# Two more blocks of the dilated values by quads of half products, and the combinations of x formed piece by piece

## The chip, the cores and the metric

The kernel runs on one core of one Trainium2 chip. The metric is the device time of one execution in microseconds (us), as the median over several runs. The engines are TensorE (PE in the rows; its weight loads are PEld), VectorE (DVE), ScalarE (ACT), GpSimd (POOL) and SyncE (SP), each of which takes its own instructions in the order in which they stand.

## The reference

A trunk of two layers over 512 tokens of width 1024, all in f32: forgetting attention with 16 heads, then dilated window attention with 3 groups of 8 heads of width 128, each followed by a gated embedding, and a norm at the end. The change lies in the input projection of the dilated layer:

```python
def dilated_mixer(h, w_in, w_out):
    B, S, _ = h.shape
    proj = h @ w_in
    shp = (B, S, DIL_GROUPS, DIL_HEADS_PER_GROUP, DIL_HEAD_DIM)
    q = proj[..., :DIL_QKV].reshape(shp)
    k = proj[..., DIL_QKV:2 * DIL_QKV].reshape(shp)
    v = proj[..., 2 * DIL_QKV:3 * DIL_QKV].reshape(shp)
    z = proj[..., 3 * DIL_QKV:]
```

The values v of a group are a product of x (512 tokens by 1024 features, after the norm) with 1024 columns of `w_in`.

## The kernel before

Every f32 operand of a projection is split into a rounded part and a remainder (`whi` and `wlo` for weights; x has the same two parts in the pair of tiles `xn2T`), and a product is three matmuls: high by high, high by low, low by high. ScalarE makes the high part of a weight, VectorE the low part by a subtraction.

The dilated layer runs in two halves, `hf` 0 and 1, of four heads each. A half begins with three blocks of values, one for each group g, of 512 columns each, called (hf, g) here; then come, for each of its four heads j, the queries and keys of three groups (`pair_rows`), and in places gates (`gate_rows`). There are two ways to compute a block of values:

- `token_rows`: the plain product. Four granules of weights (256 features by 512 columns), and for each granule four blocks of 128 tokens; one unit is 6 matmuls of 128x512, so a block is 96 of them. The four sums lie in four PSUM banks, and are copied to `v` by VectorE (even ones, line 1059) and ScalarE (odd ones, line 1057) after the last granule.
- `quad_rows`: a Strassen-like scheme, with seven half products in place of eight. `Stream.quad` makes seven combinations of the quarters a11, a12, a21, a22 of the weight block (VectorE sums of lines 144, 145, 149 and 156) and splits each of them (lines 135 and 136). Each of seven products is 24 matmuls of 128x256, so a block is 168 of them. The products are called after the parts of x that they take: "11", "t2", "t1", "t3", "21", "t4", "22", in this order. Sums between products go through three temporaries p1, u2, u4 in `ozf`.

The parts t1 to t4 of x are combinations of its four quarters. `combine_x` forms them once: four sums of high and low parts into `xf`, four differences, and four splits into the pair of tiles `comb` (12 steps on VectorE, 4 on ScalarE). Before the change it is called after the blocks (0, 0) and (0, 1) were issued, and `QUADS` names the blocks (0, 2), (1, 1) and (1, 2); the queries, keys and gates use `comb` too.

A scheduler orders the instructions of each engine from this program by what it reckons to be ready; the order in the program is only its priority. `Side` holds short pieces of work that are run at a later unit (`tick`); `chain` holds the generators of a head's scores and values (`dil_scores`, `dil_values`), of which `drive` runs a step after each unit. A generator's step ends at a `yield`.

Two things that the prediction also speaks of: at the start of the layer GpSimd builds three tables of distances, `d0`, `d1` and `d2` (lines 861 to 872; the last takes 32 selects one after the other), and VectorE makes from them the biases of each head (lines 911 to 913, in `dil_scores`), those of head 0 being free to run as soon as the tables are there. And the scores of a head send row sums to DRAM and back (`own` to `sta` and `stb`, then to `oth`) through SyncE's queue, in which the weight loads (line 73, at most three raw granules at a time) stand too; `dil_values` turns them into the factors `alpha` (lines 969 to 977), scales the probabilities (lines 980 and 981), transposes them (line 995) and multiplies with the values (lines 1006 to 1012).

Of the kernel before, what the change touches and what calls it, by code (L numbers as in the profile page):

```python
# [19 lines left out]
OP = mybir.AluOpType  # L20
# [8 lines left out]
def f32(ap):  # L29
    return ap.bitcast(F32)  # L30
# [3 lines left out]
def trunk_kernel(ctx, tc, x, p, fox_norm, fox_w_in, fox_b_f, fox_w_out, dil_norm, dil_w_in,  # L34
                 dil_w_out, ple_w_up, ple_w_gate, final_norm, out):
    nc = tc.nc
    PE, ACT, DVE, POOL, SP = nc.tensor, nc.scalar, nc.vector, nc.gpsimd, nc.sync
# [158 lines left out]
    g_fo = [tok_granules(fox_w_out[0], c * 512) for c in range(2)]  # L196
    g_g0 = [tok_granules(ple_w_gate[0], c * 512) for c in range(2)]
    g_up1 = [ws.add(ple_w_up[1], 0, 2, c * 512, 512) for c in range(2)]
    QUADS = ((0, 2), (1, 1), (1, 2))
    g_dv, g_dq, g_dk, g_dz = {}, {}, {}, {}  # L200
    z_after = {0: (0, 1), 2: (2, 3), 4: (4, 5), 7: (6, 7)}
    for hf in range(2):
        for g in range(3):
            c0 = 6144 + g * 1024 + hf * 512
            if (hf, g) in QUADS:
                g_dv[hf, g] = [ws.add(dw, k, 4, c0 + c, 256) for k, c in ((0, 256), (0, 0), (4, 256), (4, 0))]
# [34 lines left out]
    side = Side()  # L241
# [3 lines left out]
    def step(n=1):  # L245

        for _ in range(n):
            while chain:
                try:
                    next(chain[0])  # L250
                    break
                except StopIteration:
                    chain.popleft()

    def drive(main, steps=1, at={}):


        for i, _ in enumerate(main):
            side.tick()
            step(steps if isinstance(steps, int) else steps[i])  # L260
            if i in at:
                at[i]()
# [116 lines left out]
    def quad_rows(xb, i0, pool, temps, v):  # L379

        combos = ws.quad(i0, pool)
        ready = deque()
        b1, b2, b3, b4 = (rotate(mm) for _ in range(4))
        p1, u2, u4 = temps

        def dst(cols, h):
            return v[:, 2 * h:2 * h + 2, 256 * cols:256 * cols + 256]

        def halves(t):
            return t.rearrange("p (r c) -> p r c", r=2)  # L390

        def product(o, n, first):

            while len(ready) < 5:
                c = next(combos, None)
                if c is None:
                    break
                ready.append(c)
            wh, wl = ready.popleft()
            for r in range(2):  # L400
                oo = o[:, r * 256:(r + 1) * 256]
                for k in range(4):
                    xh, xl = (a[:, k, r * P:(r + 1) * P] for a in xb[n])
                    PE.matmul(oo, xh, wh[:, k, :], start=first and r == 0 and k == 0, stop=False,
                              skip_group_check=True)
                    PE.matmul(oo, xh, wl[:, k, :], start=False, stop=False, skip_group_check=True)
                    PE.matmul(oo, xl, wh[:, k, :], start=False, stop=(k == 3), skip_group_check=True)

        product(b1, "11", True)
        ACT.activation(p1, b1, AF.Copy)  # L410
        yield
        product(b2, "t2", True)
        DVE.tensor_tensor(u2, b2, p1, OP.add)
        yield
        product(b4, "t1", True)
        DVE.tensor_tensor(u4, b4, u2, OP.add)
        yield
        product(b3, "t3", True)
        DVE.tensor_tensor(dst(1, 1), halves(b3), halves(u4), OP.add)
        yield  # L420
        product(b1, "21", False)
        ACT.activation(dst(0, 0), halves(b1), AF.Copy)
        yield
        product(b3, "t4", False)
        DVE.tensor_tensor(dst(1, 0), halves(b3), halves(u2), OP.add)
        yield
        product(b4, "22", False)
        DVE.tensor_tensor(dst(0, 1), halves(b4), halves(u2), OP.add)
        yield

# [2 lines left out]
    def split_out(hi, lo, src):  # L433
        last["act"] = ACT.activation(hi, src, AF.Copy)  # L434
        DVE.tensor_tensor(lo, src, f32(hi), OP.subtract)
# [417 lines left out]
    dp = dil.enter_context(tc.tile_pool(name="dil", bufs=1))  # L853
    xT = xn2T[0]
# [3 lines left out]
    for r in range(4):  # L858
        d = d0[32 * r:32 * r + 32]
# [11 lines left out]
    for n in range(32):  # L871
# [9 lines left out]
    xb = {f"{i + 1}{h + 1}": [a[:, 4 * i:4 * i + 4, 256 * h:256 * h + 256] for a in xT]  # L881
          for i in range(2) for h in range(2)}
# [10 lines left out]
        return lambda h: (d[:, 256 * h:256 * h + 256], lambda t: t)  # L893

    def combine_x():
        xf = dp.tile([P, 4, 4, 256], F32, tag="ozf", bufs=1, name="xf")
        b11, b12, b21, b22 = (xf[:, i] for i in range(4))
        for n, d in (("11", b11), ("12", b12), ("22", b22), ("21", b21)):
            DVE.tensor_tensor(d, f32(xb[n][0]), f32(xb[n][1]), OP.add)
        DVE.tensor_tensor(b11, b12, b11, OP.subtract)  # L900
        DVE.tensor_tensor(b12, b22, b12, OP.subtract)
        DVE.tensor_tensor(b22, b22, b11, OP.subtract)
        DVE.tensor_tensor(b21, b21, b22, OP.subtract)
        for n, d in (("t1", b11), ("t2", b22), ("t3", b12), ("t4", b21)):
            split_out(xb[n][0], xb[n][1], d)

    def dil_scores(j, st):
        bias0 = dp.tile([P, 256], F32, tag="bias0", bufs=1, name=nm("bias0"))
# [142 lines left out]
    for hf in range(2):  # L1051
        v = [dp.tile([P, NB, 512], F32, tag=f"v{g}", bufs=1, name=nm("v"))
             for g in range(3)]
        for g in range(3):
            def dv_evac(b, t, g=g, v=v):
                if b % 2:
                    ACT.activation(v[g][:, b, :], t, AF.Copy)
                else:
                    DVE.tensor_copy(v[g][:, b, :], t)
            if hf == 0 and g == QUADS[0][1]:  # L1060
                combine_x()
                ozf = dp.tile([P, 8, T], F32, tag="ozf", bufs=1, name="ozf")
            if (hf, g) in QUADS:
                drive(quad_rows(xb, g_dv[hf, g][0], dp, [ozf[:, n, :] for n in (5, 6, 7)], v[g]))
            else:
                drive(token_rows(xT, g_dv[hf, g], blk, dv_evac))
            if g == 0:
                to_blocks(v[0])
        for j in range(4 * hf, 4 * hf + 4):
            st = {"q": [], "k": [], "v": v}  # L1070
            for g in range(3):
                views = []
                for n, nme in enumerate("qk"):
                    d = qk[:, 2 * g + n, :]
                    if g:
                        d = d.rearrange("p (r i) -> p r i", r=4)
                    st[nme].append(d)
                    views.append(by_residue(qk[:, 2 * g + n, :]) if g else by_block(d))
                drive(pair_rows(xb, g_dq[j, g], g_dk[j, g], dp, *views))
            if j < 7:  # L1080
                finish()
                chain.extend((dil_scores(j, st), dil_values(j, st)))
            else:
                chain.appendleft(dil_scores(j, st))
                chain.append(dil_values(j, st))
            if j in z_after:
                drive(gate_rows(*z_after[j]), (0,) + (1,) * 6)
# [59 lines left out]
```

## Time and profile before

| | |
|---|---|
| median of 3 runs | 967.32 us (966.49 to 968.38) |
| the profiled execution | 967.62 us, its span 965.6 us |
| granted TensorE clock, mean | 0.996 |
| TensorE busy / weight loads | 97% / 87% of the span |
| VectorE, ScalarE, GpSimd busy | 72%, 51%, 6% |
| DMA | 104.56 MB, mean 108 GB/s |

All times in rows are microseconds from the start of the span. A busy TensorE only says that its pipeline was never empty; how fast it ran shows in the distance between the starts of matmuls. The span leaves out some 2 us around it.

### The profile page before, as it was taken

The numbers are of one execution on the slowest core, as the hardware profiler recorded it, in microseconds if no ns is written. First come the engines' busy times: TensorE is split into PE (matmuls) and PEld (weight loads), VectorE is DVE, ScalarE is ACT, GpSimd is POOL, SyncE is SP. The second block draws the span as 40 slices with busy tenths as digits, with TensorE's granted clock in tenths as the row PEclk, the third lists the DMA queues.
The fourth block names the chain that finished last, engine by engine and source line by source line (L and its number), as shares of the span: only waits on it lengthen the run. The fifth ranks groups of instructions, "written<-read, shape, count | busy, mean of one in ns | idle before, by whom it ended". The sixth has DMA issues, their size and how long they took to land. (4 is left out here: it accounts for less than half of the span.)

```text
span 965.6 us, 15587 instructions
## 1 busy us (share of the span) xinstructions
PE 939.6 (97%) x5928; PEld 840.9 (87%) x5928; DVE 695.9 (72%) x1416; ACT 494.9 (51%) x915; POOL 54.7 (6%) x103
## 2 busy tenths in 40 slices
PE   6999999999999999899999999999999999999996
PEld 5888888888888888789999999999999999997885
DVE  5765877777764478758888887657888897666445
ACT  6455777777752246334464555444355455464233
POOL 0000000000010000920000000010000000000000
PEclk9999999999999999999999999999999999999998
DMA  8453222221246227253333323335332322345302
GB/s 293 124 153 88 67 67 67 66 67 66 67 153 218 87 90 259 66 154 87 113 85 88 78 77 95 104 113 147 91 110 68 110 71 72 99 156 200 128 1 87
DMA packets 127355, 104.56 MB, mean 108 GB/s; under 512 B 16528, under 2 KB 105616, under 8 KB 127280
## 3 DMA queue, kind: packets, MB, share of 16 engines
q1 hardware_dynamic: 123008, 90.65, 31.5%
q0 software_dynamic: 4096, 12.65, 3.9%
q8 instruction: 46, 0.75, 0.3%
q14 instruction: 29, 0.24, 0.1%
q10 hardware_dynamic: 176, 0.26, 0.1%
HBM read 92.93 MB, written 10.55 MB: 107 GB/s over the span
## 5 line engine op out<-in xcount | busy, mean ns | idle before, releaser
L87 DVE TENSOR_TENSOR wlo<-wraw,whi 128x1024 fp32r<-128x1024 f32 (+1 forms) x82 | 99.5, 1214 | 102.2 <-ACT whi L86 101.7
L86 ACT ACTIVATE whi<-wraw 128x1024 fp32r<-128x1024 f32 (+1 forms) x82 | 85.7, 1047 | 100.4 <-PE ps L300 62.2
L347 PE MATMUL ps<-comb,whi 128*128 128x256 f32 x448 | 131.2, 293 | 0.0
L349 PE MATMUL ps<-comb,wlo 128*128 128x256 f32 x448 | 126.8, 283 | 0.0
L348 PE MATMUL ps<-comb,whi 128*128 128x256 f32 x448 | 126.7, 283 | 0.0
L347 PE MATMUL ps<-xn2T,whi 128*128 128x256 f32 x336 | 97.1, 289 | 0.0
L349 PE MATMUL ps<-xn2T,wlo 128*128 128x256 f32 x336 | 95.0, 283 | 0.0
L348 PE MATMUL ps<-xn2T,whi 128*128 128x256 f32 x336 | 95.0, 283 | 0.0
L108 ACT ACTIVATE whi<-ws 128x1024 fp32r<-128x1024 f32 x56 | 59.2, 1057 | 68.2 <-PE ps L348 59.5
L348 PEld LDWEIGHTS ps<-comb,whi 128*128 128x128 f32 x448 | 85.8, 192 | 0.4
L347 PEld LDWEIGHTS ps<-comb,whi 128*128 128x128 f32 x448 | 85.8, 192 | 0.4
L349 PEld LDWEIGHTS ps<-comb,wlo 128*128 128x128 f32 x448 | 85.7, 191 | 0.0
L328 PE MATMUL ps<-xnT,whi 128*128 128x512 f32 x192 | 78.5, 409 | 0.0
L109 DVE TENSOR_TENSOR wlo<-ws,whi 128x1024 fp32r<-128x1024 f32 x56 | 68.4, 1221 | 11.8 <-ACT whi L108 11.6
L330 PE MATMUL ps<-xnT,wlo 128*128 128x512 f32 x192 | 75.5, 393 | 0.0
L329 PE MATMUL ps<-xnT,whi 128*128 128x512 f32 x192 | 75.1, 391 | 0.0
L108 ACT ACTIVATE whi<-wraw 128x1024 fp32r<-128x1024 f32 (+1 forms) x56 | 47.2, 843 | 34.4 <-issue 12.4
L348 PEld LDWEIGHTS ps<-xn2T,whi 128*128 128x128 f32 x336 | 64.4, 192 | 0.0
L347 PEld LDWEIGHTS ps<-xn2T,whi 128*128 128x128 f32 x336 | 64.4, 192 | 0.0
L349 PEld LDWEIGHTS ps<-xn2T,wlo 128*128 128x128 f32 x336 | 64.3, 191 | 0.0
L109 DVE TENSOR_TENSOR wlo<-wraw,whi 128x1024 fp32r<-128x1024 f32 (+1 forms) x56 | 52.8, 950 | 0.2 <-ACT whi L108 0.2
L298 PE MATMUL ps<-whi,ozT 128*128 128x512 f32 x128 | 51.0, 400 | 1.0 <-ACT ozT L434 1.0
(242 smaller groups left out, 2422.3 us busy)
## 6 DMA issues: line engine op xcount, KB each, us to landing
wraw<-in_dil_w_in_dram SPq DMA_DIRECT2D x80, 512.0 KB, 3.7
wraw<-in_fox_w_in_dram SPq DMA_DIRECT2D x32, 512.0 KB, 4.1
wraw<-in_ple_w_gate_dram SPq DMA_DIRECT2D x16, 512.0 KB, 4.1
up_dram<-upo SPq DMA_DIRECT2D x16, 256.0 KB, 3.8
wraw<-in_fox_w_out_dram SPq DMA_DIRECT2D x8, 512.0 KB, 3.5
up<-up_dram POOLq DMA_DIRECT2D x8, 512.0 KB, 8.0
wraw<-in_dil_w_out_dram SPq DMA_DIRECT2D x8, 512.0 KB, 3.5
x_in<-in_x_dram SPq DMA_DIRECT2D x4, 512.0 KB, 9.5
```

The lines of the kernel that those rows point to most:

```text
L86: ACT.activation(hi[:, k], t[:, k], AF.Copy)
L87: DVE.tensor_tensor(lo[:, k], t[:, k], f32(hi)[:, k], OP.subtract)
L108: ACT.activation(hi[:, :n], src, AF.Copy)
L109: DVE.tensor_tensor(lo[:, :n], src, f32(hi[:, :n]), OP.subtract)
L298: PE.matmul(o, xh, wh[:, kk, c0:c1], start=first, stop=False)
L328: PE.matmul(t, wh[:, k, :], xh, start=(k == 0), stop=False)
L329: PE.matmul(t, wh[:, k, :], xl, start=False, stop=False)
L330: PE.matmul(t, wl[:, k, :], xh, start=False, stop=(k == KT - 1))
L347: PE.matmul(o, ah, bh, start=(first and k == 0), stop=False, skip_group_check=not first)
L348: PE.matmul(o, ah, bl, start=False, stop=False, skip_group_check=not first)
L349: PE.matmul(o, al, bh, start=False, stop=(last and k == 3), skip_group_check=not first)
```

## The change

`QUADS` also names (0, 1) and (1, 0), so that only (0, 0) remains a plain product. `product` in `quad_rows` now yields after its first half too, so a quad has 14 units in place of 7, and `drive` runs two steps of `chain` after each unit of the block (1, 0). `combine_x` no longer issues its steps at once: it returns a list of 12 pieces, of which one is pushed for each unit of the plain product (0, 0), and what is left is issued behind it.

```diff
-    QUADS = ((0, 2), (1, 1), (1, 2))
+    QUADS = ((0, 1), (0, 2), (1, 0), (1, 1), (1, 2))
...
+                if r == 0:
+                    yield
...
-        product(b1, "11", True)
+        yield from product(b1, "11", True)
...
     def combine_x():
+
         xf = dp.tile([P, 4, 4, 256], F32, tag="ozf", bufs=1, name="xf")
         b11, b12, b21, b22 = (xf[:, i] for i in range(4))
-        for n, d in (("11", b11), ("12", b12), ("22", b22), ("21", b21)):
-            DVE.tensor_tensor(d, f32(xb[n][0]), f32(xb[n][1]), OP.add)
-        DVE.tensor_tensor(b11, b12, b11, OP.subtract)
-        DVE.tensor_tensor(b12, b22, b12, OP.subtract)
-        DVE.tensor_tensor(b22, b22, b11, OP.subtract)
-        DVE.tensor_tensor(b21, b21, b22, OP.subtract)
-        for n, d in (("t1", b11), ("t2", b22), ("t3", b12), ("t4", b21)):
-            split_out(xb[n][0], xb[n][1], d)
...
+        return [total("11", b11), total("12", b12), total("22", b22), less(b11, b12, b11),
+                less(b12, b22, b12), parts("t1", b11), less(b22, b22, b11), parts("t2", b22),
+                total("21", b21), parts("t3", b12), less(b21, b21, b22), parts("t4", b21)]
...
-            if hf == 0 and g == QUADS[0][1]:
-                combine_x()
+            if (hf, g) in QUADS:
+                drive(quad_rows(xb, g_dv[hf, g][0], dp, [ozf[:, n, :] for n in (5, 6, 7)], v[g]),
+                      2 if g == 0 else 1)
+            else:
+                for n, piece in enumerate(combine_x()):
+                    side.push(piece, n)
+                drive(token_rows(xT, g_dv[hf, g], blk, dv_evac))
+                side.flush()
                 ozf = dp.tile([P, 8, T], F32, tag="ozf", bufs=1, name="ozf")
-            if (hf, g) in QUADS:
-                drive(quad_rows(xb, g_dv[hf, g][0], dp, [ozf[:, n, :] for n in (5, 6, 7)], v[g]))
-            else:
-                drive(token_rows(xT, g_dv[hf, g], blk, dv_evac))
             if g == 0:
                 to_blocks(v[0])
```

Where this puts the instructions is the scheduler's doing, and three places of its order matter. All line numbers of the program with the change are higher, by 2 in its first half and by 8 from the biases on.

The first place is VectorE's order where the first quad begins; the biases are the three rows of `bias`. Before, with the block (0, 1) a plain product whose weights are the `wlo` of line 87, and the first combination of (0, 2) in line 144:

```order
L903 TENSOR_TENSOR xf<-xf 128x1024
L435 TENSOR_TENSOR comb_3562<-xf,comb_3561 128x1024
L87 TENSOR_TENSOR wlo_3768<-wraw_3708,whi_3767 128x1024
L1059 COPY v_3563<-ps_3566 128x512
L435 TENSOR_TENSOR comb_3562<-xf,comb_3561 128x1024
L1059 COPY v_3563<-ps_3586 128x512
L912 TENSOR_SCALAR bias_679_4497<-dist_3431 128x128
L913 TENSOR_SCALAR bias_679_4497<-dist_3432 128x128
L144 TENSOR_TENSOR ws_3853<-wraw_3741,wraw_3797 128x1024
L136 TENSOR_TENSOR wlo_3850<-wraw_3771,whi_3849 128x1024
```

With the change, where `wlo_3730` belongs to the second product ("t2") of the quad (0, 1), `wlo_3734` to its third and `wlo_3744` to its fourth; `ps_3567` and `ps_3590` are two banks of the plain product:

```order
L437 TENSOR_TENSOR comb_3562<-xf,comb_3561 128x1024
L145 TENSOR_TENSOR ws_3726<-ws_3725,wraw_3646 128x1024
L1067 COPY v_3563<-ps_3567 128x512
L919 TENSOR_SCALAR bias_687_4590<-dist_3430 128x256
L920 TENSOR_SCALAR bias_688_4591<-dist_3431 128x128
L921 TENSOR_SCALAR bias_688_4591<-dist_3432 128x128
L136 TENSOR_TENSOR wlo_3730<-ws_3726,whi_3729 128x1024
L1067 COPY v_3563<-ps_3590 128x512
L136 TENSOR_TENSOR wlo_3734<-ws_3725,whi_3733 128x1024
L149 TENSOR_TENSOR ws_3737<-wraw_3646,wraw_3610 128x1024
L136 TENSOR_TENSOR wlo_3744<-ws_3737,whi_3743 128x1024
L156 TENSOR_TENSOR ws_3726<-wraw_3739,ws_3726 128x1024
```

The bias that reads the last table stood behind all four weights of the block that ran next; it now stands behind the weights of one product (`wlo_3722`, further up) and ahead of those of the other six.

The second place is VectorE's order while head 3's factors are formed, in the block (1, 0). Before:

```order
L149 TENSOR_TENSOR ws_6407<-wraw_6291,wraw_6249 128x1024
L969 TENSOR_TENSOR alpha_6311<-own_6190,oth_6191 128x8
L970 TENSOR_TENSOR alpha_6311<-alpha_6311,own_6190 128x8
L971 TENSOR_TENSOR alpha_6311<-alpha_6311,oth_6191 128x8
L973 TENSOR_TENSOR alpha_6311<-alpha_6311,own_6190 128x8
L974 TENSOR_TENSOR alpha_6311<-alpha_6311,oth_6191 128x8
L975 TENSOR_TENSOR alpha_6311<-alpha_6311 128x8
L976 RECIPROCAL alpha_6311<-alpha_6311 128x8
L977 TENSOR_TENSOR alpha_6311<-alpha_6311 128x8
L980 TENSOR_SCALAR p_946_6188<-p_946_6188,alpha_6311 128x128
```

With the change:

```order
L977 TENSOR_TENSOR alpha_6435<-own_6313,oth_6314 128x8
L145 TENSOR_TENSOR ws_6616<-ws_6615,wraw_6401 128x1024
L978 TENSOR_TENSOR alpha_6435<-alpha_6435,own_6313 128x8
L979 TENSOR_TENSOR alpha_6435<-alpha_6435,oth_6314 128x8
L136 TENSOR_TENSOR wlo_6620<-ws_6616,whi_6619 128x1024
L981 TENSOR_TENSOR alpha_6435<-alpha_6435,own_6313 128x8
L982 TENSOR_TENSOR alpha_6435<-alpha_6435,oth_6314 128x8
L136 TENSOR_TENSOR wlo_6624<-ws_6615,whi_6623 128x1024
L983 TENSOR_TENSOR alpha_6435<-alpha_6435 128x8
L149 TENSOR_TENSOR ws_6627<-wraw_6401,wraw_6284 128x1024
L984 RECIPROCAL alpha_6435<-alpha_6435 128x8
L985 TENSOR_TENSOR alpha_6435<-alpha_6435 128x8
```

Four steps of the next quad's weights now stand between the steps of the factors.

The third place is SyncE's queue there. Before, and then with the change:

```order
L955 DMA sta_6257<-own_6190 32x4x2 x4
L957 DMA oth_6191<-sta_6257 128x8
L955 DMA stb_6258<-own_6190 32x4x2 x4
L958 DMA oth_6191<-stb_6258 128x8
L73 DMA wraw_6409<-in_dil_w_in_dram 128x4x256
```

```order
L963 DMA sta_6376<-own_6313 32x4x2 x4
L73 DMA wraw_6401<-in_dil_w_in_dram 128x4x256
L963 DMA stb_6377<-own_6313 32x4x2 x4
L965 DMA oth_6314<-sta_6376 128x8
L73 DMA wraw_6404<-in_dil_w_in_dram 128x4x256
L966 DMA oth_6314<-stb_6377 128x8
```

Two weight loads, which wait for a free granule, now stand ahead of parts of the round trip.

## Rows read from the trace of the kernel before

**Rows 1.** The page: busy time of each engine in the whole span.

```profile
PE 939.6 (97%) x5928; PEld 840.9 (87%) x5928; DVE 695.9 (72%) x1416; ACT 494.9 (51%) x915; POOL 54.7 (6%) x103
```

**Rows 2.** Waits, 379 to 450 us: who waited for whom, total us, times, longest.

```profile
DVE bias L913 <- POOL dist L872: 7.8, 1, 7.8
...
PE ps L298 <- DVE v L1059: 2.8, 1, 2.8
```

**Rows 3.** Timeline of TensorE, blocks (0, 0) to (0, 2): start, length, instruction.

```profile
378.95 0.47 PE L298 MATMUL ps<-whi,xn2T 128*128 128x512 f32 x1
...
400.60 0.39 PE L300 MATMUL ps<-whi,xn2T 128*128 128x512 f32 x1
403.79 0.47 PE L298 MATMUL ps<-whi,xn2T 128*128 128x512 f32 x1 [2.81 <-DVE v L1059]
...
427.28 0.28 PE L404 MATMUL ps<-whi,xn2T 128*128 128x256 f32 x1
...
447.43 0.28 PE L347 MATMUL ps<-xn2T,whi 128*128 128x256 f32 x1
```

**Rows 4.** Stretches: TensorE, PEld, VectorE, ScalarE, GpSimd busy, granted clock, DMA share, GB/s.

```profile
405.00:406.00 1.00, 1.00 (x3) 0.73 (x3) 0.51 (x2) 0.00 (x0) 0.86 (x3) 0.50 0.98 340
...
408.00:409.00 1.00, 1.00 (x6) 0.83 (x5) 0.00 (x0) 0.00 (x0) 0.79 (x4) 1.00 0.00 0
```

**Rows 5.** Timeline of VectorE, 383 to 414 us.

```profile
383.24 5.11 DVE L899 TENSOR_TENSOR xf<-xn2T,xn2T 128x1024 f32<-128x1024 f32 x4 [0.21 <-DVE wlo L87]
...
393.02 0.29 DVE L911 TENSOR_SCALAR bias<-dist 128x256 f32<-128x256 f32 x1 [1.91 <-POOL dist L864]
...
398.05 1.31 DVE L435 TENSOR_TENSOR comb<-xf,comb 128x1024 fp32r<-128x1024 f32 x1
399.28 1.31 DVE L903 TENSOR_TENSOR xf<-xf 128x1024 f32<-128x1024 f32 x1
...
402.97 0.68 DVE L1059 COPY v<-ps 128x512 f32<-128x512 f32 x1
...
405.30 0.21 DVE L912 TENSOR_SCALAR bias<-dist 128x128 f32<-128x128 f32 x1
413.32 0.23 DVE L913 TENSOR_SCALAR bias<-dist 128x128 f32<-128x128 f32 x1 [7.81 <-POOL dist L872]
413.46 1.22 DVE L144 TENSOR_TENSOR ws<-wraw,wraw 128x1024 f32<-128x1024 f32 x1
```

**Rows 6.** Timeline of GpSimd, 380 to 400 us (its last row is cut there).

```profile
387.35 2.69 POOL L864 TENSOR_SCALAR_AFFINE_SELECT dist<-dist 32x256 f32<-32x256 f32 x2
...
390.97 0.97 POOL L862 TENSOR_SCALAR_AFFINE_SELECT dist<-dist 32x256 f32<-32x256 f32 x2
...
394.56 6.18 POOL L872 TENSOR_SCALAR_AFFINE_SELECT dist<-dist 128x128 f32<-128x128 f32 x5
```

**Rows 7.** Line 872: its 32 selects, length in ns least/median/most, first and last start.

```profile
L872 POOL TENSOR_SCALAR_AFFINE_SELECT dist<-dist x32: 293/295/1302, 394.6 to 413.0; 128x128 f32<-128x128 f32 x32
```

**Rows 8.** VectorE's timeline at 427 us: the quad's fourth granule.

```profile
427.60 1.23 DVE L156 TENSOR_TENSOR ws<-wraw,ws 128x1024 f32<-128x1024 f32 x1 [2.59 <-DMA wraw<-in_dil_w_in_dram]
```

**Rows 9.** The page's DMA issues: number, KB each, median us to landing.

```profile
wraw<-in_dil_w_in_dram SPq DMA_DIRECT2D x80, 512.0 KB, 3.7
```

**Rows 10.** TensorE's timeline in the block (1, 0).

```profile
614.32 0.40 PE L298 MATMUL ps<-whi,xn2T 128*128 128x512 f32 x1
...
638.17 0.49 PE L995 MATMUL ps<-ident,p 128*128 128x128 f32 x3
...
643.83 0.38 PE L404 MATMUL ps<-whi,xn2T 128*128 128x256 f32 x1
```

**Rows 11.** VectorE's timeline there: the factors.

```profile
632.40 0.16 DVE L969 TENSOR_TENSOR alpha<-own,oth 128x8 f32<-128x8 f32 x1
634.04 1.07 DVE L980 TENSOR_SCALAR p<-p,alpha 128x128 f32<-128x128 f32 x4
```

More of the change, by code (lines that the diff above doesn't have):

```diff
@@ L407, in product @@
                     PE.matmul(oo, xl, wh[:, k, :], start=False, stop=(k == 3), skip_group_check=True)
-        product(b1, "11", True)
+                if r == 0:
+                    yield
+        yield from product(b1, "11", True)
         ACT.activation(p1, b1, AF.Copy)
         yield
-        product(b2, "t2", True)
+        yield from product(b2, "t2", True)
         DVE.tensor_tensor(u2, b2, p1, OP.add)
         yield
-        product(b4, "t1", True)
+        yield from product(b4, "t1", True)
         DVE.tensor_tensor(u4, b4, u2, OP.add)
         yield
-        product(b3, "t3", True)
+        yield from product(b3, "t3", True)
         DVE.tensor_tensor(dst(1, 1), halves(b3), halves(u4), OP.add)
         yield
-        product(b1, "21", False)
+        yield from product(b1, "21", False)
         ACT.activation(dst(0, 0), halves(b1), AF.Copy)
         yield
-        product(b3, "t4", False)
+        yield from product(b3, "t4", False)
         DVE.tensor_tensor(dst(1, 0), halves(b3), halves(u2), OP.add)
         yield
-        product(b4, "22", False)
+        yield from product(b4, "22", False)
         DVE.tensor_tensor(dst(0, 1), halves(b4), halves(u2), OP.add)
@@ L897, in combine_x, with total, less, parts @@
         b11, b12, b21, b22 = (xf[:, i] for i in range(4))
-        for n, d in (("11", b11), ("12", b12), ("22", b22), ("21", b21)):
-            DVE.tensor_tensor(d, f32(xb[n][0]), f32(xb[n][1]), OP.add)
-        DVE.tensor_tensor(b11, b12, b11, OP.subtract)
-        DVE.tensor_tensor(b12, b22, b12, OP.subtract)
-        DVE.tensor_tensor(b22, b22, b11, OP.subtract)
-        DVE.tensor_tensor(b21, b21, b22, OP.subtract)
-        for n, d in (("t1", b11), ("t2", b22), ("t3", b12), ("t4", b21)):
-            split_out(xb[n][0], xb[n][1], d)
+        def total(n, d):
+            return lambda: DVE.tensor_tensor(d, f32(xb[n][0]), f32(xb[n][1]), OP.add)
+        def less(d, a, b):
+            return lambda: DVE.tensor_tensor(d, a, b, OP.subtract)
+        def parts(n, d):
+            return lambda: split_out(xb[n][0], xb[n][1], d)
+        return [total("11", b11), total("12", b12), total("22", b22), less(b11, b12, b11),
+                less(b12, b22, b12), parts("t1", b11), less(b22, b22, b11), parts("t2", b22),
+                total("21", b21), parts("t3", b12), less(b21, b21, b22), parts("t4", b21)]
     def dil_scores(j, st):
```

## The prediction

> **What bounds the kernel now.** I read the page's busy times first. TensorE is busy 97% of the span, and no other engine over 72% [rows 1]; so the time falls only if TensorE's work gets less or one of its few holes closes, and it rises if a new hole opens. The waits come next: between 379 and 450 us TensorE has one hole, 2.8 us before the first matmul of the block (0, 1), and VectorE has one of 7.8 us that nobody pays for, waiting with a bias for GpSimd's last table [rows 2]. TensorE's timeline gives the prices of the blocks [rows 3]: (0, 0) from its first start at 378.95 to its last at 400.60 is 21.65 us for 95 steps, 0.228 us a matmul and 21.9 us a block; the quad (0, 2) from 427.28 to 447.43 is 20.15 us for 168, 0.120 us each, 2.88 us a product. The block (0, 1) took 23.5 us (403.79 to 427.28), 1.6 over the price, since after the hole the granted clock was at 0.50, the lower of its two levels (1.2 GHz), and back at 1.00 only by 408 [rows 4].
>
> **The change, part by part.**
>
> *Two blocks become quads.* Each saves 21.9 - 20.15 = 1.75 us of TensorE, 3.5 in all, as long as its weights are ready.
>
> The weight loads in a quad come as often as the matmuls, every 0.120 us, and don't slow them: 168 of 256 columns took 20.15 us [rows 3]. The Trainium skill ("TensorE: Matmul & The Clock Gate", section Back-to-back issue gap) speaks against narrow matmuls: loads and matmuls set the distance together, 81 ns at 128 columns and 131 at 512. A line between these puts 256 columns at an estimated 98 ns, 16.4 us a quad against 12.6 a plain block: 3.9 us dearer, and the two would make the total 11 us longer than my sum. The rows have both shapes and say otherwise, and they decide.
>
> *The combinations of x* are the same 12 steps on VectorE and 4 on ScalarE, and still fill VectorE while (0, 0) runs: 4 sums in 5.11 us, and 1.23 from one step to the next later on [rows 5]. The quad's first weights take the place of three granules of (0, 1).
>
> *The old hole before (0, 1)* goes: 400.83 to 403.79 idle and 1.6 of low clock, 4.6 us. In its place the quad waits for one copy out of a bank, which stands behind 14 steps of about 1.25 us: 383.24 + 17.5 = 400.7, and the copy 0.6 more. So the first product runs from some 401.4 to 404.3.
>
> *The second product then waits, and this is the term that decides.* Its low weights stand on VectorE behind the bias that reads the last table. In the trace this bias started at 413.32, after 7.81 us of waiting [rows 5]; it cost nothing, since the four granules of (0, 1) stood ahead of it and fed TensorE until 427. Now one product of 2.9 us stands ahead of it. When is the table there? GpSimd is slow while VectorE works: its first five selects took 6.18 us, 1.24 each [rows 6], and alone a select takes 0.295 [rows 7]. By 405.3 about 8.7 were done (10.7 / 1.24), and the other 23.3 took the 8.0 us to 413.3, 0.34 each. With the change VectorE reaches the wait earlier, at 401.7 in place of 405.3, which speeds GpSimd up earlier; but the 1.9 us in which VectorE waited for the first table [rows 5], and GpSimd made two pairs of selects in 0.97 us each, not 2.69 [rows 6], are gone, so that the 32 selects begin some 3.4 us later, at 397.9. By 401.7 three are done; 29 x 0.34 = 9.9 more end at 411.6. Bias 0.2 and split 1.2: the second product goes on at **413.2**. Bounds: had GpSimd been alone from 390, the selects would end about 405; if VectorE keeps it back as long as before plus the late start, at 415. I take the middle because both rates come from this very loop.
>
> *From there:* six products are 17.3 us. The clock after a stop of 9 us I price by the one after the 3 us stop: about 3.8 us at half speed, 1.9 lost. The fourth granule (a12) is requested only after the sum of line 149; its data came 2.6 us late for VectorE in the trace [rows 8], though a granule takes 3.7 us as a rule [rows 9], and nobody waited. That sum would end at 416, the data be there at 420 to 421 and split at 423, when the fifth product wants it: 0.5 us for this and the next quad's first weights. So (0, 1) ends at 413.2 + 17.3 + 1.9 + 0.5 = 432.9 and (0, 2) at 453.1, against 447.43: **+5.7 us**. VectorE keeps up after that: a quad needs 11 steps of at most 1.22 us and 5 of 0.68 [rows 5], 16.8 us in 20.
>
> *The block (1, 0)* before: 614.32 to 643.83 with head 3's scores, transposes and values, 29.5 us, no wait [rows 10]. It saves 1.75. Against it: the factors of head 3 started at 632.40 and the probabilities were scaled from 634.04 on [rows 11], 1.6 us later; now four steps of 1.2 us for the next quad stand between, which makes it 6.4, and 7.5 with the scaling. The round trip through DRAM has two weight loads ahead of its second half; I leave its end at 632, as the scores come a little earlier (two steps of the chain a unit). The probabilities are then scaled by 639. TensorE, with five more products of (1, 0) and one of (1, 1) to do, is through with those at about 637.6: it waits 1.4, then some 1 for the copies of the transposes (two banks), and some 2 before the product "t4", whose bank must first be read into `v`, behind a split that waits for the next granule. Some 1.9 of this stands against the old order's own time. I take 2.4 us lost, 1.75 gained: **+0.6**; bounds -1.75 (everything hidden) and +6 (all of it late, with a fall of the clock).
>
> *Sum:* +5.7 + 0.6 = +6.3 on the profiled execution's 967.62, which lies 0.3 over the median of 967.32. I predict **973.6 us**. A measurement of this kernel can tell about 0.2% (1.9 us) from no change.
>
> **The rivals.**
>
> *The table is there in time, or is no bound* (faster). Then the quad (0, 1) runs from 401.4 to 421.6 and (0, 2) to 441.7, 5.7 us earlier than before, and (1, 0) gives 1.75: 967.3 - 7.4 = 959.9. For it: VectorE stops early, and GpSimd then has the time to itself. Against it: the trace shows the table at 413, and its 32 selects alone need over 10 us. It decides if the selects end before 404. Chance 0.09.
>
> *About nothing.* The selects end near 406 to 408 because VectorE stands still so early; the wait is 3 us, the clock costs 1.5, and both are paid by the old hole and by 3.5 us of saved products: 966 to 969. Chance 0.09.
>
> *Head 3's factors cost more.* The late round trip (its second half behind a granule that VectorE frees late) and the four steps between put the transposes at 643 in place of 638; with the clock's fall this is +6 in (1, 0): 979. For it: the order; against it: one product of (1, 1) was drawn ahead of the transposes. Chance 0.13.
>
> *Narrow matmuls don't pay.* If the loads of the new quads were not hidden, the distance would be more than 0.120 us; each 0.01 costs 1.7 a block. The three quads of the trace show none of it: chance 0.01.
>
> **How the numbers follow.** My forecast has the other 0.68, with 971 to 977 as its own range (the selects' end from 410 to 413.5, (1, 0) from -1.75 to +2). The range of **968.5 to 980** takes in the third rival and the upper part of the second, and leaves out the first and some tails. Faster by over 0.2%: the first rival and a little of the second, 0.11; within 0.2%: 0.08; slower: 0.81.
>
> **What would show it.** In the profile after: VectorE's wait at line 921 for GpSimd, ending near 411.6, and right behind it TensorE's wait of about 9 us at the second product of the first quad, with the clock at 0.50 after it. No hole before the first quad over 1 us. Quads of 20.2 us without waits. In (1, 0), waits of TensorE at the transposes of some 1 to 3 us. I am wrong if TensorE runs through the first quad, which would put the total near 960, or if the loss lies elsewhere than at that bias.

## The result and the profile after

The change made the kernel slower: **983.12 us** (981.9 to 986.41, four runs) against 967.56 for the kernel before beside it, a ratio of 1.0167 with an interval of 1.014 to 1.0194. The profiled execution took 981.9 us, its span 980.2, at a mean granted clock of 0.991. The forecast was 973.6, with a range to 980.

The page's busy times, against [rows 1]: TensorE is busy as long as before (slow matmuls after a stop count in full), in a span 14.6 us longer. So the time went into holes and into those matmuls.

```profile
PE 939.9 (96%) x6072; PEld 848.0 (87%) x6072; DVE 715.7 (73%) x1436; ACT 499.4 (51%) x921; POOL 53.2 (5%) x103
```

The waits of after, 379 to 460 us (who waited for whom, total us, times, longest), against [rows 2]:

```profile
DVE bias L921 <- POOL dist L874: 9.3, 1, 9.3
PE ps L406 <- DVE wlo L136: 7.8, 1, 7.8
PE ps L404 <- DVE v L421: 2.4, 1, 2.4
PE ps L404 <- DVE v L1067: 1.9, 1, 1.9
```

VectorE's wait at the bias, which cost nothing before, now has a wait of TensorE behind it; and there is a stop before the product "t4" (the bank that line 421 reads), which I had reckoned with in (1, 0) only. TensorE's timeline of after, against [rows 3]:

```profile
402.39 0.35 PE L404 MATMUL ps<-whi,xn2T 128*128 128x256 f32 x1 [1.88 <-DVE v L1067]
...
413.41 0.58 PE L406 MATMUL ps<-wlo,comb 128*128 128x256 f32 x1 [7.79 <-DVE wlo L136]
...
433.31 0.28 PE L404 MATMUL ps<-whi,xn2T 128*128 128x256 f32 x1
...
439.89 0.36 PE L404 MATMUL ps<-whi,comb 128*128 128x256 f32 x1 [0.65 <-DVE v L430]
...
451.16 0.36 PE L404 MATMUL ps<-whi,comb 128*128 128x256 f32 x1 [2.41 <-DVE v L421]
...
456.99 0.28 PE L347 MATMUL ps<-xn2T,whi 128*128 128x256 f32 x1
```

The second product resumed at 413.41 (forecast 413.2) and (0, 1) ended at 433.31 (forecast 432.9). The quad (0, 2) then took 23.7 us in place of 20.15, so that the queries and keys of head 0 begin at 456.99: 9.6 us later than before, where I had 5.7.

VectorE's timeline shows both causes. First the bias of line 921, which ends its wait at 412.00 (GpSimd's 32 selects of line 874 ran from 396.85 to 411.97), and the split behind it; then the end of (0, 2):

```profile
402.37 0.31 DVE L920 TENSOR_SCALAR bias<-dist 128x128 f32<-128x128 f32 x1
412.00 0.23 DVE L921 TENSOR_SCALAR bias<-dist 128x128 f32<-128x128 f32 x1 [9.32 <-POOL dist L874]
412.14 1.22 DVE L136 TENSOR_TENSOR wlo<-ws,whi 128x1024 fp32r<-128x1024 f32 x1
...
442.83 1.23 DVE L156 TENSOR_TENSOR ws<-wraw,ws 128x1024 f32<-128x1024 f32 x1 [1.25 <-DMA wraw<-in_dil_w_in_dram]
...
448.60 1.22 DVE L109 TENSOR_TENSOR wlo<-wraw,whi 128x1024 fp32r<-128x1024 f32 x1
449.73 0.68 DVE L114 TENSOR_TENSOR ws<-wraw 128x512 f32<-128x512 f32 x1
450.33 0.68 DVE L421 TENSOR_TENSOR v<-ps,ozf 128x512 f32<-128x512 f32 x1
```

The sum of line 156 waits for its granule, and the whole chain of the quad's splits and sums shifts with it. The step of line 421, which frees the bank that "t4" needs, stands behind two steps for the next pair (lines 109 and 114), 1.7 us that VectorE has no time for any more. The quad's weights were late before that: two of its first granules, asked for at 422.47 and 423.60, landed 5.7 and 7.3 us later, beside the four transfers that bring v of (0, 0) back from DRAM (the last of them landed at 426.79). GpSimd's timeline, and the DMA issues from 422.4 to 424 us (number, KB each, median us to landing):

```profile
418.03 2.20 POOL L1055 DMA_DIRECT2D v<-vd  x4 [2.71 <-DMA vd<-v]
...
wraw<-in_dil_w_in_dram SPq DMA_DIRECT2D x2, 512.0 KB, 6.5
```

The clock after the long stop, in stretches (columns as in [rows 4]): half speed until 419.

```profile
409.00:413.40 4.40, 0.00 (x0) 0.00 (x0) 1.40 (x3) 0.00 (x0) 3.53 (x11) 0.53 0.03 10
413.40:416.00 2.60, 2.59 (x12) 2.59 (x13) 2.57 (x3) 0.00 (x0) 1.07 (x2) 0.50 0.76 282
416.00:419.00 3.00, 3.00 (x16) 3.00 (x16) 1.58 (x2) 1.54 (x2) 0.97 (x2) 0.50 0.70 221
419.00:420.00 1.00, 1.00 (x9) 1.00 (x8) 0.00 (x0) 0.00 (x0) 1.00 (x3) 0.76 1.07 372
420.00:423.00 3.00, 3.00 (x28) 3.00 (x27) 2.92 (x3) 2.92 (x3) 0.23 (x1) 1.00 1.09 278
```

The second place is (1, 0) and (1, 1). TensorE's waits of after, 612 to 703 us:

```profile
PE ps L404 <- ACT whi L135: 2.7, 1, 2.7
PE ps L404 <- DVE v L421: 0.9, 1, 0.9
PE ps L406 <- DVE wlo L136: 0.9, 1, 0.9
PE ps L1003 <- ACT pt L1006: 0.4, 1, 0.4
```

The largest is at the product "t2" of (1, 1), whose weights wait for its third granule, a22, not at the transposes of head 3 (0.4 us), where I had looked for it. A half clock from 652 to 655 follows. SyncE's queue of after shows what ran beside that granule:

```profile
634.37 0.39 SPq L73 DMA_DIRECT2D wraw<-in_dil_w_in_dram  x1
635.91 1.73 SPq L963 DMA_DIRECT2D stb<-own  x4
637.75 0.36 SPq L965 DMA_DIRECT2D oth<-sta  x1
638.16 0.43 SPq L73 DMA_DIRECT2D wraw<-in_dil_w_in_dram  x1
```

The DMA issues of after from 634.3 to 646 us (number, KB each, median us to landing):

```profile
wraw<-in_dil_w_in_dram SPq DMA_DIRECT2D x2, 512.0 KB, 7.3
stb<-own SPq DMA_DIRECT2D x4, 1.0 KB, 6.0
```

The same view of the kernel before, 611 to 631 us:

```profile
wraw<-in_dil_w_in_dram SPq DMA_DIRECT2D x3, 512.0 KB, 3.8
stb<-own SPq DMA_DIRECT2D x4, 1.0 KB, 2.2
```

Beside the exchange of row sums a granule takes twice its time. The blocks (1, 0) to (1, 2) took 76.15 us (625.68 to 701.83) against 71.75 before: +4.4, forecast +0.6. Head by head the sum closes: +9.6 at 457, +1.8 in the heads 0 to 3, +4.4 in the second half's blocks, -1.4 in the heads 4 to 7, +0.2 in the rest, 14.6 us of span. The profiled execution is the shortest of the four; the median is 1.2 us higher, and no trace shows where.

### The profile page after: what moved, and what is told of

Same layout as the page of the kernel before. It is cut to its first block, busy times and chain, and to the rows that moved or that the text cites. A ratio compares the mean times of both kernels' runs of the same rounds, so it can differ in the third digit from the quotient of the medians.

```text
span 980.2 us, 15906 instructions
## 1 busy us (share of the span) xinstructions
PE 939.9 (96%) x6072; PEld 848.0 (87%) x6072; DVE 715.7 (73%) x1436; ACT 499.4 (51%) x921; POOL 53.2 (5%) x103
## 4 chain that ended last, share of the span: by engine, by line
PE 71%; DVE 10%; DMA 8%; ACT 4%; issue 3%; POOL 3%; SPq 1%; POOLq 0%; DVEq 0%; ACTq 0%
PE ps L347 8%; PE ps L348 8%; PE ps L349 8%; PE ps L298 6%; PE ps L300 6%; PE ps L299 6%; PE ps L328 4%; PE ps L330 4%; PE ps L329 4%; DMA wraw<-in_dil_w_in_dram 3%; PE ps L712 2%; PE ps L1020 1%; PE ps L1003 1%; DVE wlo L136 1%; POOL dist L874 1%
## 5 line engine op out<-in xcount | busy, mean ns | idle before, releaser
L87 DVE TENSOR_TENSOR wlo<-wraw,whi 128x1024 fp32r<-128x1024 f32 (+1 forms) x74 | 89.3, 1208 | 99.6 <-ACT whi L86 99.1
L86 ACT ACTIVATE whi<-wraw 128x1024 fp32r<-128x1024 f32 (+1 forms) x74 | 77.2, 1046 | 91.4 <-PE ps L300 59.3
L108 ACT ACTIVATE whi<-wraw 128x1024 fp32r<-128x1024 f32 (+1 forms) x56 | 47.2, 843 | 30.4 <-issue 11.0
L406 PE MATMUL ps<-wlo,comb 128*128 128x256 f32 x160 | 47.4, 296 | 8.7 <-DVE wlo L136 8.7
L404 PE MATMUL ps<-whi,comb 128*128 128x256 f32 x160 | 47.5, 297 | 6.7 <-DVE v L421 3.3
```

The lines of the kernel that those rows point to most:

```text
L86: ACT.activation(hi[:, k], t[:, k], AF.Copy)
L87: DVE.tensor_tensor(lo[:, k], t[:, k], f32(hi)[:, k], OP.subtract)
L108: ACT.activation(hi[:, :n], src, AF.Copy)
```

## The experiments

The kernel before ran beside each, with medians between 967.3 and 969.7 us, so the runs are compared by ratios. All are made from the changed kernel.

**Each part alone.** The pieces without new quads, then one new quad at a time:

```diff
-    QUADS = ((0, 1), (0, 2), (1, 0), (1, 1), (1, 2))
+    QUADS = ((0, 2), (1, 1), (1, 2))           # e4
+    QUADS = ((0, 1), (0, 2), (1, 1), (1, 2))   # e2
+    QUADS = ((0, 2), (1, 0), (1, 1), (1, 2))   # e3
```

(In all runs in which (0, 1) or (1, 0) is plain, `combine_x` runs in (0, 0) alone.)

> Neither block is a quad; only the combinations of x are formed piece by piece between the units of (0, 0), and the product of a quad may be interrupted after its first half. Theory: the same 12 steps fill VectorE in the same time, so no difference from the kernel before: 967 to 968.5 us. Rival (the pieces make the first weights of (0, 1) later, or the halves of a product let late work in): 970 to 973.

Measured: 968.31 us, ratio 0.9997 (0.9985 to 1.0009). The pieces cost nothing, as the forecast had it.

> The changed kernel with (1, 0) as a plain product again, (0, 1) still a quad. Theory (two separate losses): the loss up to the pairs after (0, 2) stays at +9.6 us, that of the stretch from (1, 0) to (1, 2), which was +4.4 in the trace, goes; so 977 to 979 us. Rival 1 (the second loss only follows from the shift in time of everything before): 982 to 984. Rival 2 (the whole loss is in the first half): also 982 to 984, but then with (1, 0) unchanged beside the kernel before.

Measured: 977.99 us, 1.0096 (1.0078 to 1.0114). The bias's wait is there again (7.8 us of TensorE), and the stop before "t4" as well (2.2). In this execution the pairs begin at 459.73, 2.7 us later than in after, with a half clock from 453.1 to 456.5 that after does not have.

> The changed kernel with (0, 1) as a plain product again, (1, 0) still a quad; the combinations of x are still formed piece by piece beside (0, 0). Theory: no stop at the table, since four granules of (0, 1) stand ahead of the bias; the loss from (1, 0) to (1, 2) stays, +3 to +4.4 us: 970.5 to 972. Rival (the block's own price was +0.6, as predicted, and the rest came from (0, 1)): 967.5 to 968.5.

Measured: 971.91 us, 1.0035 (1.0021 to 1.0048). The ten executions took from 968.4 to 973.4 us, and the profiled one is the shortest. In it the blocks (1, 0) to (1, 2) took 76.17 us, as in after. Its waits, 612 to 703 us, have the stop at "t2" of (1, 1) longest:

```profile
PE ps L404 <- ACT whi L135: 3.6, 1, 3.6
```

So both quads lose, and about as the trace of after says: 1.0096 and 1.0035 make 1.0131 of 1.0167; 3.5 us remain that neither part shows alone.

**The bias out of the way.**

```diff
+        def far():
             DVE.tensor_scalar(bias1[:, P:], d2, -slope(2, j) / scale, None, OP.mult)
+        if j == 0:
+            with tc.issue_after(last["sum"].ins):
+                far()
```

> The changed kernel, with one edit: head 0's bias from the last table is issued behind the sums of the pair before its scores, no longer ahead of the second product's low weights. Theory (the wait for GpSimd's table is the main loss): the 7.8 us stop of TensorE and the about 3.2 us of low clock behind it go, so 983.1 - 11 = 972 us, and the pairs after (0, 2) start near 446 in place of 457. Rival 1 (something else is late right behind it, such as the fourth granule or VectorE's own 14 steps): only about half comes back, 977 to 979. Rival 2 (the low weights were late anyway): 982 to 984.

Measured: 975.28 us, 1.0074 (1.0059 to 1.0089). The stop at the table is gone, so the first half of the theory holds; but the head's pairs begin at 452.02, not before 447. The waits of this run, 379 to 460 us, show why:

```profile
PE ps L404 <- DVE v L421: 4.9, 1, 4.9
```

Behind this stop the granted clock was at 0.50 up to 448.5.

VectorE's timeline in this run, end of (0, 2):

```profile
441.82 1.22 DVE L109 TENSOR_TENSOR wlo<-wraw,whi 128x1024 fp32r<-128x1024 f32 x1 [2.27 <-ACT whi L108]
442.97 0.68 DVE L114 TENSOR_TENSOR ws<-wraw 128x512 f32<-128x512 f32 x1
443.57 0.68 DVE L421 TENSOR_TENSOR v<-ps,ozf 128x512 f32<-128x512 f32 x1
```

The pair's first split stands ahead of line 421 in VectorE's list and waits for a granule that was asked for at 428.94 and landed at 440.63, 11.7 us later. GpSimd's timeline tells what it shared the DMA engines with:

```profile
397.66 25.23 POOL L874 TENSOR_SCALAR_AFFINE_SELECT dist<-dist 128x128 f32<-128x128 f32 x32
...
428.23 2.21 POOL L1061 DMA_DIRECT2D v<-vd  x4 [3.21 <-DMA vd<-v]
```

`to_blocks` sends v of (0, 0) to DRAM and back in eight transfers on GpSimd's queue, in another arrangement, behind the selects of the table. These now end at 422.90, since VectorE works on where it used to wait: 15 of the 32 took 1.16 to 1.31 us, beside VectorE's two-input steps, and 17 took 0.29 to 0.37. The Trainium skill ("GPSIMD Engine Reference", section Key points) says that GpSimd shares its SBUF interfaces with VectorE and contends with VectorE instructions that have two SBUF inputs; this trace agrees, at a factor of four.

**The read first, and the table last.** e5 puts the whole pair's VectorE steps behind line 421; e6 leaves them and puts the 32 selects behind the eight transfers. Both keep e1's edit.

```diff
-        a11, a12, a22, s1, s2, s3, s4 = ws.pair(ia, ib, pool)
+        with read_first():                        # e5
+            a11, a12, a22, s1, s2, s3, s4 = ws.pair(ia, ib, pool)
...
+    def far_table(behind):                        # e6
+        with tc.issue_after(behind.ins):
+            POOL.memset(d2, BIG)
```

> As e1, and the steps on VectorE for the first pair after (0, 2) are issued behind the read of the bank into v (line 421), no longer ahead of it. In e1 TensorE stood 4.9 us before the product t4 of (0, 2), since VectorE waited with the pair's split for a granule that came 11.7 us after its request, and the read stood behind that split. Theory (order on VectorE): the stop shrinks to under 1 us and the low clock after it goes, so 975.3 - 5 = 970 us (969 to 971.5). Rival (the late granule itself is the bound): the stop moves to the first products of the pair, 974 to 976.

Measured: 976.98 us, 1.0107 (1.0069 to 1.0144). The stop before "t4" fell to 1.3 us and the pairs begin at 447.52, 4.5 earlier than in e1; but the heads 0 to 3 took 171.2 us against 166.9 before, and the gain was lost there.

> As e1, and GpSimd makes the last table (32 selects) behind the eight transfers that rearrange v[0], no longer ahead of them. Theory (the granule of e1 is late because those transfers, pushed to 423 to 440 us by the slow selects, share the DMA engines with it): they run about 10 us earlier, the granule takes 4 to 6 us, and the stop before t4 falls from 4.9 to about 2 us: 972 to 973.5 us. Rival (the order on VectorE alone, or the granule is late for its request): 975 to 976.

Measured: 972.76 us, 1.0054 (1.0035 to 1.0072). The stop fell to 2.6 us and the pairs begin at 447.09, 4.9 earlier than in e1. The transfers were through at 417.05, and the granule that took 11.7 us in e1 took 6.0. So they had delayed it, as the theory had it.

**What delays the granule in the second half.** With (1, 0) as the only new quad, three edits: the exchange on GpSimd's queue; head 3's exchange left out; one step of the chain a unit, not two.

```diff
-                SP.dma_start(d.rearrange("(m i) n s -> i m n s", m=4)[:, :, n, :],
+                POOL.dma_start(d.rearrange("(m i) n s -> i m n s", m=4)[:, :, n, :],   # e7
...
+        if j == 3:                                                                     # e10
+            DVE.tensor_copy(oth[:, 4:8, :], own[:, 0:4, :])
+            DVE.tensor_copy(oth[:, 0:4, :], own[:, 4:8, :])
+            return
...
-                      2 if g == 0 else 1)
+                      1)                                                               # e11
```

> As e3 (of the two blocks only (1, 0) is a quad), and the exchange of each head's factors through DRAM is issued by GpSimd's queue, no longer by SP's between the granules. Theory (the third granule of (1, 1) is late, since its request stands behind the exchange of head 3 on SP and its transfer took 7.2 us beside it): TensorE's stop of 3.6 + 0.7 us in (1, 1) goes to under 1, with the low clock behind it: 971.9 - 5 = 967 us (966 to 968.5). Rival 1 (the scaling of the probabilities is late anyway): the stop moves to the transposes, 970.5 to 972. Rival 2 (GpSimd's requests are slower and other heads lose by it): over 972.

Measured: 971.70 us, 1.0050 (1.0027 to 1.0073). The granule still took 8.1 us (626.56 to 634.66) and the stops of 2.5 and 0.9 stay, with one of 1.4 at head 3's transposes. So it isn't the order in SyncE's queue: beside the exchange the granule is slow whichever queue issues the exchange.

> As e3 (of the two blocks only (1, 0) is a quad), with head 3's exchange of factors through DRAM left out: both halves of the partners' factors are copied on VectorE from the head's own, so head 3's probabilities are scaled by other numbers. Theory (the granules of (1, 1) are late since they share the DMA queues with the exchange's packets of 8 bytes: 7 to 8 us from request to landing in place of 3.7): TensorE's stop of 3.6 + 0.7 us before the product t2 of (1, 1) goes, with the low clock after it: 971.9 - 5 = 967 us (966 to 968). Rival (the granules are late because VectorE frees their buffers late, or SP asks late): the stop stays, 971 to 972.5.

Measured: 967.25 us, 0.9977 (0.9966 to 0.9988), against 969.71 before. The DMA issues of this run, 621 to 630 us:

```profile
wraw<-in_dil_w_in_dram SPq DMA_DIRECT2D x2, 512.0 KB, 3.6
```

The granules land in half the time, the stop at "t2" is gone, and (1, 0) to (1, 2) took 70.18 us, 1.57 less than before: nearly all of the 1.75 that a quad saves. The exchange is the cause: the edit also takes away the wait for the factors, but the stop at "t2" was one for a granule. It moves packets of 8 bytes; the Trainium skill ("DMA: Bandwidth & Descriptors", section Specifications) says that transfers under 512 bytes make the engine read, modify and write. The runs show the 3.6 and the 7.3 us, not whether this is the reason.

> As e3, but one step of head 3's chain per unit of (1, 0), not two. Theory (the exchange collides with whichever granules are under way, and a later exchange makes the scaling later): head 3's scores come some 5 us later, the stop at t2 of (1, 1) shrinks, but the transposes and values come later and the bank of t4 is free later: 971 to 975 us. Rival (the two steps a unit are what put the exchange on top of the granules): 967 to 969.

Measured: 970.02 us, 1.0001 (0.9989 to 1.0012), against 969.71. (1, 0) to (1, 2) took 71.78 us, 4.4 less than with two steps, so the rival came true and not the theory. The two steps a unit had put the exchange onto the granules; with one, the quad comes out as the plain block did.

**All mended at once.** e8 takes the edits of e1, e5, e6 and e7 with both quads; e9 those of e1 and e6, with only the split of line 109 behind the read, and (1, 0) plain.

```diff
-                DVE.tensor_tensor(lo[:, :n], src, f32(hi[:, :n]), OP.subtract)
+                later(lambda: DVE.tensor_tensor(lo[:, :n], src, f32(hi[:, :n]), OP.subtract))   # e9
```

> The changed kernel with all four edits: the bias behind the sums, the read of the bank first, the table behind the rearrangement, and the exchange on GpSimd's queue. Theory (the losses are these four and they add up): 983.1 - 11 - 5 - 5 = 962 us (960 to 965), faster than the kernel before, with the two quads' 3.5 us and the old hole of (0, 1) as the gain. Rival (one bound is left each time, such as VectorE's 17 us of work in a block of 20): 966 to 970.

Measured: 980.52 us, 1.0128 (1.0098 to 1.0159). A miss: the pairs begin at 445.32, earlier than before, but the heads 0 to 3 took 174.8 us. TensorE waited there twice for the scaling of the probabilities, 4.2 us in all, with 3.4 us at half clock after one of these stops. From its first transfer to its last landing the exchange of the heads 0 to 2 took 13.8 to 15.9 us on GpSimd's queue, against 13.0 to 13.2 on SyncE's in after, though a single part landed as fast (median 1.7 against 1.9).

> Only (0, 1) is a quad beside the three of before; head 0's bias is issued behind the sums of the pair (as e1), GpSimd's last table behind the rearrangement of v[0] (as e6), and of the first pair after (0, 2) one step alone, the low half of its first split, behind the read of the bank into v. Theory (with these waits gone the quad is worth what the trace says: 1.75 us of products and part of the old hole): the pairs after (0, 2) start 3 to 3.5 us earlier than in the kernel before, 444 in place of 447.4, and the rest is as before: 964 to 964.5 us. Rival (VectorE's order in the following pairs shifts as in e5, where heads 0 to 3 took 4 us longer): 967 to 969.

Measured: 971.72 us, 1.0027 (1.0016 to 1.0039). A miss: the stop before "t4" is still 3.2 us, the pairs begin at 451.34.

**The late fourth granule, and the transfers beside it.** In e12 the difference a11 - a21 goes into a spare part of `ozf` ahead of the splits, so that the quad's fourth granule can be asked for earlier; it keeps the edits of e1, e5 (for (0, 2)) and e6, with (1, 0) plain. e13 is the same with both quads and one step a unit.

```diff
+            if spare is not None:
+                DVE.tensor_tensor(spare, a11, a21, OP.subtract)
+                self.prefetch(i0 + 4)
             DVE.tensor_tensor(s2, s1, a11, OP.subtract)
```

> Only (0, 1) is a quad beside the three of before; bias behind the sums (e1), table behind the rearrangement (e6), the first pair's steps on VectorE behind the read of the bank (e5), and, in the first half, the difference a11 - a21 is formed in a free part of ozf before the two splits, so that SP asks for the fourth granule some 4 us earlier. Theory (in e9 and in the changed kernel that granule, asked for only when the third product's weights are formed, comes late and bunches VectorE's work, until the read before t4 is 2.4 to 3.2 us late): no stop at t4 over 1 us, the pairs after (0, 2) start by 444.5, 3 us earlier than in the kernel before; ratio to it 0.996 to 0.998. Rival 1 (VectorE has no room in a quad that follows a quad, whenever its data come): the stop stays at 2 us or more, ratio 1.000 to 1.003. Rival 2 (the heads' pairs lose it again, as 4 us in e5): pairs start by 444.5, but ratio 1.000 or more.

Measured: 971.62 us, 1.0037 (1.0025 to 1.0050). The quad (0, 2) ran 20.2 us without a stop, which was the aim. But (0, 1) now stops 7.9 us before its own "t4". Its DMA issues, 411.5 to 424 us:

```profile
v<-vd POOLq DMA_DIRECT2D x4, 256.0 KB, 8.6
...
wraw<-in_dil_w_in_dram SPq DMA_DIRECT2D x1, 512.0 KB, 11.2
```

VectorE's timeline there:

```profile
423.10 1.33 DVE L144 TENSOR_TENSOR ws<-wraw,wraw 128x1024 f32<-128x1024 f32 x1 [6.07 <-DMA wraw<-in_dil_w_in_dram]
424.36 0.68 DVE L430 TENSOR_TENSOR v<-ps,ozf 128x512 f32<-128x512 f32 x1
```

The next quad's granule takes 11.2 us beside the four transfers back; the sum that waits for it stands ahead of the read that frees the bank. It is the pattern of e1 one block earlier.

> As e12, with (1, 0) a quad too and one step of head 3's chain per unit of it (e11). Theory (the losses are the waits, each at its place): as e12, and from (1, 0) to (1, 2) 71.7 us as in e11 and in the kernel before, so the same ratio as e12, 0.996 to 0.998. Rival: (1, 0) costs 3 us as in e3, ratio 1.000 to 1.001 where e12 has 0.997.

Measured: 976.17 us, 1.0087 (1.0073 to 1.0100). A miss: the same stop, 6.5 us, and (1, 0) to (1, 2) took 73.1 us, not 71.7.

**The rearrangement spread out.** e14 is e12 with the eight transfers issued by SyncE one at a time, each behind a granule of head 0's pairs, where nothing needs v yet, and with the quad's read ahead of the next quad's weights. The table's selects stay where they were. e15 adds the quad (1, 0) with one step a unit. The code shows the transfers alone.

```diff
+        def out(r):
+            with tc.issue_after(last["load"].ins):
+                SP.dma_start(d[r], v[:, r, :])
...
+        for n, step_ in enumerate((out, back)):
+            for r in range(NB):
+                side.push(lambda step_=step_, r=r: step_(r), 2 + 3 * (NB * n + r))
```

> As e12 (only (0, 1) is a quad beside the three of before), but the eight transfers that rearrange v[0] are issued by SP, one at a time behind the granules of head 0's pairs, and each quad's read of its bank into v stands ahead of the next quad's weights on VectorE. Theory (in e12 the stop of 7.9 us before t4 of (0, 1) came from a granule that took 11.3 us beside those transfers): both quads run at 20.2 us with no stop over 1 us after the first product, and the pairs start at 443 to 444.5 in place of 447.4; ratio to the kernel before 0.9955 to 0.9975. Rival 1 (the quads have no room for their weights whatever the transfers do): stops of 2 us or more stay, ratio 1.000 to 1.004. Rival 2 (the pairs' granules are now late): pairs start by 444.5, head 0 loses 3 us or more, ratio 0.999 to 1.003.

Measured: **963.48 us against 967.66, ratio 0.9965 (0.9952 to 0.9978)**: faster than both kernels. The only wait of TensorE from 379 to 460 us is the one before the first quad:

```profile
PE ps L416 <- DVE v L1102: 2.0, 1, 2.0
```

Its granules, 403 to 417 us, land in 4.2 us:

```profile
wraw<-in_dil_w_in_dram SPq DMA_DIRECT2D x4, 512.0 KB, 4.2
```

TensorE's timeline has the two quads in 41.9 us, and the pairs at 444.40, 3.0 us earlier than [rows 3]:

```profile
402.52 0.36 PE L416 MATMUL ps<-whi,xn2T 128*128 128x256 f32 x1 [2.01 <-DVE v L1102]
...
444.40 0.28 PE L357 MATMUL ps<-xn2T,whi 128*128 128x256 f32 x1
```

Of the 4.1 us of span that e14 gains, 3.0 lie ahead of the pairs; the heads 0 to 3 lost 1.2, the blocks (1, 0) to (1, 2) gained 0.9 and the heads 4 to 7 gained 1.3, and why was not tried. Nor does e14 tell apart its two edits, the later transfers and the read put first.

> As e14, with (1, 0) a quad too and one step of head 3's chain per unit of it (e11). Theory: (1, 0) to (1, 2) take 71.7 us as in the kernel before, so the ratio is that of e14 within 0.001. Rival: its transfers and the exchange cost 2 to 3 us more than in e14.

Measured: 968.54 us, 1.0016 (1.0000 to 1.0031). The first half is better still, with the pairs at 441.69, to the tenth of a microsecond the time of the forecast's first rival:

```profile
441.69 0.28 PE L357 MATMUL ps<-xn2T,whi 128*128 128x256 f32 x1
```

But (1, 0) to (1, 2) took 73.1 us, with a stop of 1.9 at head 3's transposes, the heads 0 to 3 took 168.5, and the rest was longer too. The version to keep is e14, with (1, 0) left plain.

## Why the forecast was wrong, point by point

- **The sign and the main mechanism were right.** The second product waits for the last table: VectorE's bias at 412.00 (411.6), TensorE at 413.41 (413.2), the first quad's end at 433.31 (432.9). (The terms 411.6 + 0.2 + 1.2 make 413.0, not 413.2.) e1 removes that wait by one edit and it goes.
- **The clock after that stop** was under-priced: the 28 matmuls up to 419.5 started 0.213 us apart and not 0.120, 2.7 us lost in place of 1.9. I had taken the time at half speed after a 3 us stop [rows 4].
- **The step that failed: "0.5 us for this and the next quad's first weights", and with it "VectorE keeps up after that … 16.8 us in 20".** The late a12 cost (0, 1) nothing. It was (0, 2) that paid: two stops of 0.65 and 2.41 us, +3.5 with some 0.2 for each restart. The sum of 16.8 us was right as a load, and wrong as an argument: a list in which the read that frees a bank stands behind two steps for the next pair, and the chain starts with a granule that lands at 442.8, is late in spite of a share of 84%. The experiments show it: with the granule at 11.7 us the stop was 4.9 (e1), with it at 6.0 it was 2.6 (e6), with the read put first 1.3 (e5), and in e14, with both mended, it was gone. Moving one of the two steps from ahead of the read was not enough (3.2 in e9).
- **The second step that failed: "I leave its end at 632" and the place of the loss in (1, 0).** I looked at the order of the round trip in SyncE's queue and gave it and the granules no effect on each other's duration. The round trip landed at 645.72, 20.0 us after the start of (1, 0), against 18.0 before (and 632 with 7.5 on it makes 639.5, not 639). The exchange slows the granules from 3.6 to 7.3 us (e10), wherever it is issued (e7), and the loss was at "t2" of (1, 1), 2.7 + 0.9 us, with 1.5 us of half clock behind it: +4.4 for the blocks in place of +0.6. The third rival ("Head 3's factors cost more") came nearer with its +6, by another mechanism: in after the transposes waited 0.4 us (1.9 in e11 and e15, with one step a unit).
- **"No hole before the first quad over 1 us"** was wrong: 1.88 us. I had the copy out of the bank at 400.7; line 1067 ran at 401.57, as seven of the 14 steps ahead of it, beside GpSimd's first tables, came 1.38 us apart and not 1.25.
- **The saving of 1.75 us a quad** holds: e10 gives 1.57 with the exchange out of the way, and the 336 matmuls of e14's two quads took 41.9 us: 40.3 at 0.120 us each, and 1.5 for the half clock at the start. The Trainium skill ("TensorE: Matmul & The Clock Gate", section Back-to-back issue gap) gave the prediction its estimate of 98 ns at 256 columns; this trace does not agree, and the measurement decides.
- **The heads 0 to 3** were given no change. They took 166.9 us before, 168.7 in after and 166.7 to 174.8 in the runs, most in e8. e3, e10 and e11 have the same instructions there in the same order on TensorE, VectorE, ScalarE and SyncE, and yet took 167.8, 169.3 and 170.6: TensorE's waits in this stretch were 0.9, 2.3 and 3.1 us, and the exchange of head 0 took 12.0, 13.3 and 13.4 us from its first transfer to its last landing. So differences of 1 to 3 us in these heads can lie between executions and not in an edit; why stays open, and with it the cause of the +1.8 in after.
- **The sum.** The span grew by 14.6 us and not by 6.3. Of the 8.3 between them 3.9 lie ahead of the pairs, 3.8 in (1, 0) to (1, 2) and 0.6 in the rest.

## What to carry to other kernels

When a block gets shorter, price not only its engine but each transfer that now falls beside its loads: here a round trip of 1 MB made a 512 KB load up to three times as long, and an exchange of 8 KB in 8-byte packets twice as long. In a queue that runs in order, a read that frees a bank must stand ahead of every step that waits for data; a low busy share doesn't excuse a wrong place. And removing the first wait (e1) only shows the second: reckon the whole chain to the next stage before calling a wait the price.

## What the runs showed of the hardware

- A 512 KB granule landed in 3.6 to 3.8 us as a rule (medians), in 7.3 beside the exchange of 8-byte packets, and in up to 11.7 beside the transfers of v back from DRAM (7.3 in after, 11.2 in e12, 11.7 in e1).
- A select on GpSimd took 0.29 us, or 1.16 to 1.31 beside VectorE's steps with two inputs from SBUF; beside those with one of the two in PSUM it stayed at 0.29 (e1).
- The length of a stop did not tell whether the clock fell. After 2.01 us, in e14, the granted clock was 0.62 over the next 4.5 us:

```profile
402.50:407.00 4.50, 4.48 (x25) 4.50 (x26) 4.50 (x5) 3.29 (x5) 4.23 (x5) 0.62 0.50 150
```

After 2.27 us at the same place in e13 it stayed at 1.00:

```profile
402.20:407.00 4.80, 4.80 (x40) 4.80 (x41) 4.80 (x5) 3.28 (x5) 2.21 (x4) 1.00 0.65 187
```

Which of the two a run gets cost or spared some 1.5 us in the experiments above, and its cause was not tried.
